# Sums of MLP weight blocks: VectorE's adds replaced by accumulating DMAs on GpSimd's queue

## The chip, the cores and the metric

The program runs on one core of a Trainium2 chip. The time is the device time of one execution in microseconds (us); smaller is better. Each run of a kernel gives one such time, and one further execution is recorded by the hardware profiler.

## The reference

One layer of an encoder on a sequence of 1024 positions and 1024 channels, all in float32. The change touches only its second half, the output projection, the MLP and the last norm:

```
x = x + g1 * (merged @ w_out)
h2 = rmsnorm(x, norm2_g) * (1 + sc2) + sh2
f = square(relu(h2 @ w_ff1)) @ w_ff2        # 1024 -> 4096 -> 1024
x = x + g2 * f
out = rmsnorm(x, final_g)
```

## The kernel before

**Phases.** The first half of the program (up to about 930 us) makes `merged`. The second half, `phase2`, is nine stages of 1024x1024 matrix products: stage 0 is `merged @ w_out`; then come four pairs, an "nl" stage (one quarter of `w_ff1`, then relu and square; stages 1, 3, 5, 7) and a "lin" stage (one quarter of `w_ff2`; stages 2, 4, 6, 8).

**Seven products in place of eight.** In stages 1 to 8 both operands are cut in 2x2 quadrants, and a Strassen-like scheme makes the result from seven quadrant products. For it the weight quadrants 11, 12, 21 and 22 are combined to four sums (`WSUM`): S1 = 21 + 22, S2 = S1 + 11, S3 = 11 + 21, S4 = S2 + 12 (signs are already in the weights). Each sum is made in two halves h = 0 and 1, as tiles of 128x1024 float32 (512 KB). That makes 4 sums x 2 halves x 8 stages = 64 adds, made by `w2_add` on VectorE (L105). The tiles are eleven buffers named `wr`. When `plan` says that an input isn't needed any more, the sum is written over it (40 of the 64); otherwise it goes to a free buffer (24).

**Granules.** A product is worked in two halves, called granules J here (`self.gran[J]`): 24 matmuls of 128x512. Stage 1 is J = 16 to 29, stage 2 is J = 30 to 43, and so on by 14, stage 8 is J = 114 to 127. Each operand is split in a high and a low part, since a product is made of three matmuls (high x high, high x low, low x high): ScalarE copies the tile to `whi` or `xhi`, then VectorE subtracts to get `wlo` or `xlo` (`w2_split`, `x2_split`). Each of these four has four buffers, so granule J's split can start when granule J - 4 is done.

**Order.** Each engine runs its instructions in program order. The loop at L1727 writes, for each granule G: its matmuls; the loads of weights that become possible (SyncE's queue); `w2_add` for the next granules; the sums of x (`x2_add`); `w2_split(G + 3)`; x splits; and `x2_load(G + 3)`. The x operands of stage 1 are also written to DRAM scratch `hop` by DMAs from GpSimd's queue (L1539), and stages 3, 5 and 7 load them back from there, on the same queue (L1546), two DMAs a granule. The residual x is saved to `xsp` by that queue, too (L1597). GpSimd waits for a DMA's semaphores before it issues it, so a DMA that waits holds up those behind it.

In stage 1, `S4` is the operand of granules 20 and 21, `S2` of 22 and 23, `S3` of 24 and 25, `S1` of 26 and 27. In stage 2 `S3` is that of 32 and 33, `S2` of 34 and 35.

Of the kernel before, what the change touches and what calls it, by code (L numbers as in the profile page):

```python
# [10 lines left out]
ALU = mybir.AluOpType  # L11
# [33 lines left out]
class Program:  # L45
# [1401 lines left out]
    def w2_add(self, J):  # L1447


        s, pos, h = self.gran[J]  # L1450
        f = self.wform.get((s, h), {})
        for n, st in enumerate((self.wplan[s][pos] or ((),))[0]):
            if st[0] == "sum" and (J, n) not in self.wdone:
                _, name, a, b, at, freed = st
                if not {a, b, at or name} <= f.keys() or {at, freed} & {self.wplan[s][q][1] for q in range(pos)
                                                                     if (s, q, h) not in self.wsplit}:
                    return False
                self.wdone.add((J, n))
                dst = f[at or name]
                self.add(dst, f[a], f[b])  # L1460
                f[name] = dst
                if freed:
                    self.rawfree.append(f[freed])
        return True
# [83 lines left out]
    def phase2(self):  # L1548
# [42 lines left out]
        def take_out(i):  # L1591

            k, t = ((0, 0), (1, 0), (1, 1), (0, 1))[i]
            for m in range(4):
                upd(0, k, t, m, banks[i % 2][m])
                square(t, k, m)
            self.G.dma_start(out=xsp[k][t], in_=xg[k][t].rearrange("p c n -> p (c n)"))  # L1597
# [66 lines left out]
        def squares():  # L1664
            while late:
                a, sq = late.pop()
                self.add(a, a, sq)
# [43 lines left out]
        at = {}  # L1711
# [14 lines left out]
        n_g = len(self.gran)  # L1726
        for G in range(-4, n_g - 2):  # L1727
            if G >= 0:
                s, pos, h = self.gran[G]
                if s == 0:  # L1730
                    if G and G % 4 == 0:
                        take_out(G // 4 - 1)
                    bank, begins, ends, skip = banks[G // 4 % 2], G % 4 == 0, G % 4 == 3, False
                else:
                    n, (kind, order) = 7 * (s - 1) + pos, self.STAGES[s]
                    if h == 0:
                        take(n - 1) if n else take_out(3)
                    i, bank = order[pos], banks[n % 2]
                    skip = pos > 1 and order[pos - 2] == self.GOES_ON[kind].get(i)
                    begins, ends = h == 0 and not skip, h == 1  # L1740
                (whi, wlo), (xhi, xlo) = self.wops[G % 4], self.xop[G % 4]
                for p in range(2):
                    if p:
                        for f in at.get((G, "mid"), ()):
                            f()
                    for m in range(4):
                        o = slice(p * 512 + m * 128, p * 512 + (m + 1) * 128)
                        for c, (w, x) in enumerate(((whi, xhi), (whi, xlo), (wlo, xhi))):
                            self.mm(bank[m], w[:, o], x[:, p, :], start=begins and p == c == 0,
                                    stop=ends and p == 1 and c == 2, skip=skip)  # L1750
                for f in at.get((G, "end"), ()):
                    f()
            squares()
            self.w2_loads(G + 8)
            for J in range(max(G + 1, 0), min(G + 5, n_g)):
                self.w2_add(J)
            for J in range(G + 1, min(G + 5, n_g)):
                if J >= 0 and self.x2_own(J) and not 20 <= J < 24 and self.x2_there(J) <= G:
                    self.x2_add(J)
            if G >= -3:  # L1760
                self.w2_split(G + 3)
            for J in range(G + 1, min(G + 4, n_g)):
                if J >= 0 and self.x2_own(J) and (not 20 <= J < 24 or G >= 19) and self.x2_there(J) <= G:
                    self.x2_split(J)
            if G >= -3:
                self.x2_load(G + 3)
            self.w2_loads(G + 8)
            if 8 <= G < 16 or G > 32 and self.STAGES[self.gran[G][0]][0] == "nl" and self.gran[G][1] > 1:
                for J in range(G + 5, min(G + 9, n_g)):
                    self.w2_add(J)  # L1770


        cuts = (slice(0, 256), slice(256, 512))
# [146 lines left out]
```

## Time and profile before

| | |
|---|---|
| median of 3 runs | 1677.84 us (1677.39 to 1680.4) |
| profiled execution, its own time | 1678.33 us |
| span of its trace | 1676.6 us |
| TensorE (PE) busy | 1635.8 us, 98% of the span |
| VectorE (DVE) busy | 1253.8 us, 75% |
| ScalarE (ACT) busy | 669.7 us, 40% |
| GpSimd (POOL) busy | 74.6 us, 4% |
| mean granted clock of TensorE | 0.993 of full speed |

The span is that of the trace; the execution's own time has 1.7 us around it. An engine that is busy 98% of the span bounds the kernel, and the rest of the span is read from the places where that engine waits. Times within the trace are counted from the span's start.

### The profile page before, as it was taken

The page shows a single profiled execution, that of the slowest core. Times are in us where ns is not written, and L with a number is a line of the kernel's source. Part 1 is how long each engine was busy: PE and PEld are TensorE (multiplying, and loading weights), DVE is VectorE, ACT ScalarE, POOL GpSimd, SP SyncE. Part 2 cuts the span into 40 slices and gives each one's busy share as a digit, 9 for nine tenths or more (in the row PEclk, how much of TensorE's full clock was granted, in tenths as well). Part 3 has the DMA queues.
Part 4 walks back from the last instruction along what each step waited for, and adds up shares of the span by engine and source line. Part 5 has one row for each costly group of instructions (what it writes and reads, how often), then busy time and mean ns, then how long its engine had stood idle before and what let it go on. Part 6 is the DMA issues. An engine that isn't in the chain of part 4 may idle for free.

```text
span 1676.6 us, 19562 instructions
## 1 busy us (share of the span) xinstructions
PE 1635.8 (98%) x7480; PEld 1350.6 (81%) x7480; DVE 1253.8 (75%) x1912; ACT 669.7 (40%) x876; POOL 74.6 (4%) x130
## 2 busy tenths in 40 slices
PE   6999999999999999999999999999999999999996
PEld 4888878888878888888888888777888888888885
DVE  8889787769877875455666649899559847974896
ACT  5433323554436537552221235643243334323443
POOL 0000000000000000000000001100110021012002
PEclk9999999999999999999999999999999999999998
DMA  8421435533545444054464624661571274157102
GB/s 318 170 88 63 132 107 149 181 136 110 167 145 195 156 170 151 26 188 141 186 240 174 255 97 188 238 233 44 212 274 39 91 252 175 51 171 261 58 1 101
DMA packets 84768, 257.05 MB, mean 153 GB/s; under 512 B 9921, under 2 KB 24385, under 8 KB 83650
## 3 DMA queue, kind: packets, MB, share of 16 engines
q1 hardware_dynamic: 62274, 175.05, 30.8%
q0 software_dynamic: 17792, 67.12, 10.8%
q10 hardware_dynamic: 4608, 13.63, 2.1%
q8 instruction: 59, 0.97, 0.2%
q14 instruction: 35, 0.29, 0.1%
HBM read 199.14 MB, written 54.53 MB: 151 GB/s over the span
## 4 chain that ended last, share of the span: by engine, by line
PE 81%; DVE 11%; issue 3%; ACT 2%; DMA 2%; SPq 1%; DVEq 0%; ACTq 0%
PE pm L91 58%; PE pb L91 22%; DVE xlo L105 2%; DVE wlo L105 2%; DVE xg L122 1%; DVE fr L105 1%; DVE wr L105 1%; DVE fr L122 1%; SPq L149 1%; DMA ada<-ada 1%; DVE s L126 1%; DMA u<-zs 1%; DVE ssacc L105 1%; PE pb L96 0%; DMA lx<-zr 0%
## 5 line engine op out<-in xcount | busy, mean ns | idle before, releaser
L91 PE MATMUL pm<-act,whi 128*128 128x512 f32 x2176 | 673.1, 392 | 2.4 <-ACT act L146 2.4
L91 PEld LDWEIGHTS pm<-act,whi 128*128 128x128 f32 x2176 | 406.1, 188 | 88.3 <-ACT act L146 3.6
L91 PE MATMUL pm<-act,wlo 128*128 128x512 f32 x1088 | 419.8, 389 | 0.0
L146 ACT ACTIVATE whi<-wr 128x1024 fp32r<-128x1024 f32 x124 | 131.0, 1057 | 298.1 <-PE pm L91 128.8
L91 PEld LDWEIGHTS pm<-act,wlo 128*128 128x128 f32 x1088 | 204.4, 188 | 43.0
L105 DVE TENSOR_TENSOR wlo<-wr,whi 128x1024 fp32r<-128x1024 f32 x124 | 151.3, 1221 | 114.1 <-ACT whi L146 114.1
L91 PE MATMUL pb<-xhi,whi 128*128 128x512 f32 (+1 forms) x512 | 200.6, 392 | 5.0 <-DVE fr L105 2.7
L91 PE MATMUL pm<-xlo,whi 128*128 128x512 f32 (+1 forms) x528 | 203.8, 386 | 1.5 <-DVE xlo L105 1.5
L91 PE MATMUL pm<-xhi,whi 128*128 128x512 f32 (+1 forms) x528 | 204.6, 387 | 0.0
L91 PE MATMUL pm<-xhi,wlo 128*128 128x512 f32 (+1 forms) x528 | 203.8, 386 | 0.0
L91 PE MATMUL pb<-xlo,whi 128*128 128x512 f32 (+1 forms) x512 | 199.5, 390 | 0.6 <-DVE xlo L105 0.6
L91 PE MATMUL pb<-xhi,wlo 128*128 128x512 f32 (+1 forms) x512 | 199.2, 389 | 0.0
L146 ACT ACTIVATE whi<-wraw 128x1024 fp32r<-128x1024 f32 x74 | 78.1, 1057 | 102.7 <-PE pm L91 85.6
L91 PEld LDWEIGHTS pb<-xhi,whi 128*128 128x128 f32 x512 | 97.5, 190 | 26.2 <-issue 3.8
L91 PEld LDWEIGHTS pm<-xlo,whi 128*128 128x128 f32 x528 | 99.2, 188 | 21.9 <-DVE xlo L105 1.9
L91 PEld LDWEIGHTS pm<-xhi,whi 128*128 128x128 f32 x528 | 99.2, 188 | 20.1 <-issue 0.2
L91 PEld LDWEIGHTS pm<-xhi,wlo 128*128 128x128 f32 x528 | 99.2, 188 | 20.1
L91 PEld LDWEIGHTS pb<-xlo,whi 128*128 128x128 f32 x512 | 97.5, 190 | 21.2 <-DVE xlo L105 1.0
L91 PEld LDWEIGHTS pb<-xhi,wlo 128*128 128x128 f32 x512 | 97.5, 190 | 19.7
L105 DVE TENSOR_TENSOR wlo<-wraw,whi 128x1024 fp32r<-128x1024 f32 x74 | 90.0, 1218 | 8.0 <-ACT whi L146 7.7
L105 DVE TENSOR_TENSOR wr<-wr,wr 128x1024 f32<-128x1024 f32 x64 | 77.5, 1219 | 0.6
L146 ACT ACTIVATE xhi<-fr 128x1024 fp32r<-128x1024 f32 x54 | 56.6, 1050 | 44.4 <-DVE fr L122 23.3
(265 smaller groups left out, 1908.2 us busy)
## 6 DMA issues: line engine op xcount, KB each, us to landing
wr<-w SPq DMA_DIRECT2D x76, 512.0 KB, 4.5
ada<-ada SPq DMA_DIRECT2D x48, 512.0 KB, 6.4
xhi<-hop POOLq DMA_DIRECT2D x42, 512.0 KB, 3.6
xlo<-hop POOLq DMA_DIRECT2D x42, 512.0 KB, 4.9
wraw<-wgate SPq DMA_DIRECT2D x32, 512.0 KB, 3.9
tg<-tg ACTq DMA_DIRECT2D x24, 512.0 KB, 2.9
tl<-tg SPq DMA_DIRECT2D x24, 512.0 KB, 5.6
wraw<-win SPq DMA_DIRECT2D x20, 512.0 KB, 3.6
```

The costliest lines, as they stand in the source:

```text
L91: self.P.matmul(out=out, lhsT=lhsT, rhs=rhs, start=start, stop=stop, skip_group_check=skip)
L105: self.V.tensor_tensor(out=out, in0=a, in1=b, op=op)
L122: self.V.scalar_tensor_tensor(out=out, in0=a, scalar=s, in1=b, op0=op0, op1=op1, **kw)
L126: self.V.tensor_tensor_scan(out=out, data0=a, data1=b, initial=0.0, op0=ALU.mult, op1=ALU.add)
L146: self.A.activation(out=out, in_=a, func=f, **kw)
L149: (self.S if q == "S" else self.A).dma_start(out=out, in_=a)
```

## The change

`w2_add` issues DMAs from GpSimd's queue in place of VectorE's add. When the sum goes to a free buffer, a plain DMA copies the first input there, and a second DMA adds the other input to it (`accum_op`). When it is written over an input, one accumulating DMA does it. So 64 adds become 64 accumulating DMAs and 24 copies. The loop also offers sums up to eight granules ahead always, in place of four ahead and eight in some granules only.

```diff
@@ w2_add
                 dst = f[at or name]
-                self.add(dst, f[a], f[b])
+                if at is None:
+                    self.G.dma_start(out=dst, in_=f[a])
+                self.G.dma_start(out=dst, in_=f[a if at == b else b], accum_op=ALU.add)
                 f[name] = dst
@@ the loop over granules
             self.w2_loads(G + 8)
-            for J in range(max(G + 1, 0), min(G + 5, n_g)):
+            for J in range(max(G + 1, 0), min(G + 9, n_g)):
                 self.w2_add(J)
...
             self.w2_loads(G + 8)
-            if 8 <= G < 16 or G > 32 and self.STAGES[self.gran[G][0]][0] == "nl" and self.gran[G][1] > 1:
-                for J in range(G + 5, min(G + 9, n_g)):
-                    self.w2_add(J)
```

GpSimd's queue where stage 0 ends and stage 1 begins, before: the third and fourth save of x (`xsp`), and the stores of the x operands of granules 16 to 19.

```order
L1597 DMA xsp_7359<-xg_7320 128x2048
L1539 DMA hop_7328<-xhi_7004 128x1024
L1539 DMA hop_7329<-xlo_7005 128x1024
L1539 DMA hop_7330<-xhi_7006 128x1024
L1539 DMA hop_7331<-xlo_7007 128x1024
L1539 DMA hop_7332<-xhi_7008 128x1024
L1539 DMA hop_7333<-xlo_7009 128x1024
L1597 DMA xsp_7357<-xg_7318 128x2048
L1539 DMA hop_7334<-xhi_7010 128x1024
L1539 DMA hop_7335<-xlo_7011 128x1024
```

The same place with the change, first piece, with the semaphores that a DMA waits for (`DMASW` is a DMA of this queue, `DMAHW` one of SyncE's). The rows at L1461 are copies, those at L1462 accumulate: S1 of half 0 in `wr_3`, S2 of half 0 in `wr_4`, S1 of half 1 in `wr_7`.

```order
L1599 DMA xsp_7359<-xg_7320 128x2048 [waits DMASW2_49,DVE_49]
L1461 DMA wr_3_7309<-wr_1_7307 128x1024 [waits DMAHW3_49,DMAHW4_49,DMAHW1_49,DMAHW5_49,DMAHW0_49,Activation_49]
L1462 DMA wr_3_7309<-wr_2_7308 128x1024 [waits DMAHW2_49,DMASW7_49]
L1461 DMA wr_4_7310<-wr_3_7309 128x1024 [waits DMASW0_49,Activation_49]
L1462 DMA wr_4_7310<-wr_8_7314 128x1024 [waits DMAHW5_49,DMASW1_49]
L1461 DMA wr_7_7313<-wr_5_7311 128x1024 [waits DMAHW3_49,DMAHW4_49,DMASW3_49,DVE_49]
L1462 DMA wr_7_7313<-wr_6_7312 128x1024 [waits DMAHW4_49,DMASW4_49,DMASW3_49]
L1541 DMA hop_7328<-xhi_7004 128x1024 [waits DMASW5_49,Activation_49]
```

Six DMAs now stand between the third save and the first `hop` store, and four of them wait for the one just ahead of them. After five more `hop` stores the second piece follows: the last save, S4 and S3 of half 0 (in `wr_7149` and `wr_8`), the stores of granule 19, and S2, S4 and S3 of half 1.

```order
L1599 DMA xsp_7357<-xg_7318 128x2048 [waits DVE_49]
L1462 DMA wr_7149<-wr_4_7310 128x1024 [waits DMAHW7_49,DMASW4_49]
L1462 DMA wr_8_7314<-wr_1_7307 128x1024 [waits DMASW5_49]
L1541 DMA hop_7334<-xhi_7010 128x1024 [waits DMASW6_49,Activation_49]
L1541 DMA hop_7335<-xlo_7011 128x1024 [waits DMASW7_49,DVE_49]
L1461 DMA wr_1_7307<-wr_7_7313 128x1024 [waits DMASW5_49,DMASW0_49]
L1462 DMA wr_1_7307<-wr_7148 128x1024 [waits DMAHW6_49,DMASW1_49,DMASW0_49]
L1462 DMA wr_0_7306<-wr_1_7307 128x1024 [waits DMAHW0_49,DMASW2_49,DMASW1_49]
L1462 DMA wr_7148<-wr_5_7311 128x1024 [waits DMASW3_49]
```

This queue uses eight semaphores in turn, so S4 of half 0 (first L1462 row) also waits for the DMA eight ahead of it, the accumulation of S1 of half 1. The copy for S2 of half 1 into `wr_1` waits until S3 of half 0 has read `wr_1`.

VectorE in stage 2, ahead of granules 33 and 34:

```order
 L122 SCALAR_TENSOR_TENSOR fr_7001<-fr_7001 128x512
-L105 TENSOR_TENSOR wr_0_7306<-wr_0_7306,wr_7148 128x1024
-L105 TENSOR_TENSOR wr_5_7311<-wr_0_7306,wr_5_7311 128x1024
 L105 TENSOR_TENSOR fr_6996<-fr_6996,fr_6998 128x1024
 L122 SCALAR_TENSOR_TENSOR fr_6998<-fr_6996,fr_7002 128x1024
 L105 TENSOR_TENSOR wlo_7238<-wr_8_7314,whi_7237 128x1024
 L105 TENSOR_TENSOR xlo_7007<-sp_7324,xhi_7006 128x1024
-L105 TENSOR_TENSOR wr_1_7307<-wr_1_7307,wr_3_7309 128x1024
-L105 TENSOR_TENSOR wr_7149<-wr_1_7307,wr_7149 128x1024
 L105 TENSOR_TENSOR fr_6997<-fr_6997,fr_6999 128x1024
```

S1 and S2 of both halves leave VectorE here, and nothing else moves on it; the adds for S3 stood a few rows ahead.

## Rows read from the trace of the kernel before

**Rows 1.** The page's first part: busy time and share of the span

```profile
PE 1635.8 (98%) x7480; PEld 1350.6 (81%) x7480; DVE 1253.8 (75%) x1912; ACT 669.7 (40%) x876; POOL 74.6 (4%) x130
```

**Rows 2.** TensorE's waits from 930 us on: total us, times, longest

```profile
PE pm L91 <- DVE xg L122: 4.4, 1, 4.4
PE pb L91 <- DVE fr L105: 2.7, 1, 2.7
PE pb L91 <- DVE xg L122: 2.3, 1, 2.3
...
PE pm L91 <- DVE xlo L105: 1.5, 1, 1.5
```

**Rows 3.** Stretches: length; PE, PEld, DVE, ACT, POOL busy (instructions); clock, DMA share, GB/s

```profile
1064.00:1080.00 16.00, 12.99 (x49) 10.28 (x50) 13.07 (x14) 13.56 (x20) 3.19 (x6) 0.89 0.47 168
...
1128.00:1150.00 22.00, 18.22 (x72) 14.26 (x71) 21.90 (x24) 9.09 (x9) 0.00 (x0) 0.92 0.16 48
1150.00:1600.00 450.00, 450.00 (x1987) 372.62 (x1986) 334.68 (x358) 159.43 (x182) 44.23 (x84) 1.00 0.43 150
```

**Rows 4.** VectorE's adds of weight blocks: in all, then from 1107 to 1137 us

```profile
L105 DVE TENSOR_TENSOR wr<-wr,wr 128x1024 f32<-128x1024 f32 x64 | 77.5, 1219 | 0.6
...
L105 DVE TENSOR_TENSOR wr<-wr,wr 128x1024 f32<-128x1024 f32 x6 | 7.3, 1220 | 0.1
```

**Rows 5.** TensorE in time: first matmuls of granules 33, 34, 35; one whole product

```profile
1128.86 0.39 PE L91 MATMUL pm<-xhi,whi 128*128 128x512 f32 x1
...
1138.54 0.47 PE L91 MATMUL pb<-xhi,whi 128*128 128x512 f32 x1 [2.30 <-DVE xg L122]
...
1145.70 0.39 PE L91 MATMUL pb<-xhi,whi 128*128 128x512 f32 x1
...
1151.31 10.88 PE pm L91 x48
```

**Rows 6.** VectorE in time, stage 2

```profile
1123.53 2.48 DVE L105 TENSOR_TENSOR wr<-wr,wr 128x1024 f32<-128x1024 f32 x2
...
1129.45 1.22 DVE L105 TENSOR_TENSOR xlo<-sp,xhi 128x1024 fp32r<-128x1024 f32 x1
...
1136.51 1.22 DVE L105 TENSOR_TENSOR xlo<-fr,xhi 128x1024 fp32r<-128x1024 f32 x1
```

**Rows 7.** GpSimd's queue in time: the third save of x

```profile
1015.48 0.53 POOL L1597 DMA_DIRECT2D xsp<-xg  x1 [27.69 <-DVE xg L122]
```

**Rows 8.** ScalarE in time: the high parts of granules 20 and 21

```profile
1039.77 1.05 ACT L146 ACTIVATE whi<-wr 128x1024 fp32r<-128x1024 f32 x1
...
1054.81 1.04 ACT L146 ACTIVATE whi<-wr 128x1024 fp32r<-128x1024 f32 x1
```

**Rows 9.** DMAs issued from 1012 to 1068 us: KB each, median us to landing

```profile
hop<-xhi POOLq DMA_DIRECT2D x7, 512.0 KB, 2.9
hop<-xlo POOLq DMA_DIRECT2D x7, 512.0 KB, 3.9
...
xsp<-xg POOLq DMA_DIRECT2D x2, 1024.0 KB, 4.1
```

**Rows 10.** The end: TensorE's transposes, VectorE's reduce, TensorE's long wait

```profile
1638.03 0.60 PE L96 MATMUL pb<-ident,nrm 128*128 128x128 f32 x4
...
1639.60 0.68 DVE L130 TENSOR_REDUCE ss<-pb 128x4 f32<-128x512 f32 x1
...
1647.21 2.08 PE L91 MATMUL pm<-nrm,ones 128*128 128x512 f32 x2 [4.41 <-DVE xg L122]
```

**Rows 11.** Around stage 5: a weight load, the first load of x; loads' median landing

```profile
1297.01 0.33 SPq L149 DMA_DIRECT2D wr<-w  x1
...
1331.12 0.53 POOL L1546 DMA_DIRECT2D xhi<-hop  x1 [80.55 <-PE pm L91]
...
wr<-w SPq DMA_DIRECT2D x76, 512.0 KB, 4.5
```

**Rows 12.** DMAs issued from 1090 to 1112 us: KB each, median us to landing

```profile
hop<-xlo POOLq DMA_DIRECT2D x3, 512.0 KB, 13.3
```

## The prediction

> **What bounds the kernel now.** I read the busy times first: TensorE works 98% of the span [rows 1], so a change on another engine can win only where TensorE waits. Its list of waits shows four that end with VectorE's work on x or the residual [rows 2]. The stretches place them: the first near 1064 us (2.7 us waited), two between 1128 and 1150 us (1.5 and 2.3), one at 1647 us (4.4). In the first two of these stretches the granted clock is below 1 as well (0.89 and 0.92): after a wait TensorE is slow for a while. From 1150 to 1600 us it is busy for all 450 us [rows 3]. So of 64 adds that take 77.5 us of VectorE [rows 4], the forty in stages 3 to 7 stand beside a TensorE that never waits, and taking them away is worth nothing there. Only the rest can count.
>
> **What is removed.** *Stage 2.* Between 1107 and 1137 us VectorE does six adds, 7.3 us [rows 4], and is busy 21.9 of the 22 us after 1128 [rows 3]: it is behind. TensorE begins granule 33 at 1128.86, then waits for its low part of x, which starts on VectorE at 1129.45, behind the two adds at 1123.53; granule 34 begins at 1138.54, after the low part of 1136.51 [rows 5, 6]. Granules 33 and 34 together take 1145.70 - 1128.86 = 16.84 us, and two granules at pace 10.88 [rows 5]: the wait and the slow clock behind it cost 5.96 us. Four adds stand ahead of the first late low part, 4 x 1.22 = 4.9 us, so it starts near 1124.6, ahead of 1128.86; all six stand ahead of the second, which starts near 1129.2, while granule 34 at pace begins at 1134.3. Both are then in time, by more than 3 us. I count the whole 5.96 us as won.
>
> *Stage 1.* The wait near 1064 us follows a chain on ScalarE and VectorE with no add in it; the three adds at its head give back about 0.9 us, if the sums come in time (below).
>
> *The end.* The transposes for the last norm are done at 1638.63, and VectorE's reduce begins only at 1639.60, since VectorE is late; the long wait that ends at 1647.21 lies behind it [rows 10]. Stage 8's S4 adds (2.4 us) stand ahead of the reduce. It can't start before the transposes: I count 0.9 us.
>
> **What is added.** 88 DMAs of 512 KB on GpSimd's queue. No row shows an accumulating DMA, nor one from SBUF to SBUF. Let c be the time of a copy from issue to landing, a that of an accumulation. For c the near rows are this queue's 512 KB stores in the stretch in question, 2.9 and 3.9 us [rows 9]; I take 3.7, as more traffic is added there. For a: not below the 2.9 of a plain store; 1 MB on the same queue takes 4.1 [rows 9], and an accumulation reads twice what it writes; the upper end is twice the slower store, 7.8. I take 5.0, nearest the 1 MB row, with 0.9 for the company.
>
> A page of the Trainium skill has a price for a: "Collectives: The Full Stack", in its part on why ReduceScatter is half of AllGather, says that the add in a DMA engine costs no time of its own, only a second source read on the same ring. An estimate by that page is a near 4.2 us, and the sum below would then show no loss at all in stage 1.
>
> The sums are needed late everywhere but in stage 1. There they form one chain in the queue (the second and third order pieces). It starts when the third save of x is issued, 1015.48 + 0.53 = 1016.0 [rows 7]:
> - copy and add for S1 of half 0, then copy and add for S2: the last add is issued at 1016.0 + 2c + a;
> - half a microsecond later the copy for S1 of half 1, then its add, which lands at 1016.5 + 3c + 2a;
> - S4 of half 0 waits for that add's semaphore (same one of eight), and S3 of half 0 is issued 0.5 us behind it: it lands at 1017.0 + 3c + 3a. The `hop` stores and the save that stand between take 7 x 0.53 us and pass in the time of that add;
> - S2 of half 1: its copy needs the buffer that S3 has read (+c), its add (+a), then S4 of half 1 (+a).
>
> S4 of half 1 lands at 1017.0 + 4c + 5a = 1017.0 + 14.8 + 25.0 = 1056.8. Granule 21's high part is made from it on ScalarE, in program order, at 1054.81 before [rows 8]. So it is 2.0 us late. Queued behind it on ScalarE and VectorE are the normed x, the sums of x and the split for granule 22, the chain at whose end TensorE already waits near 1064 us: the 2.0 us pass to it whole, and the 0.9 us of stage 1 are not won. (S4 of half 0 lands at 1016.5 + 3c + 3a = 1042.6, 2.8 us after 1039.77 [rows 8]; ScalarE waits for TensorE and VectorE shortly after that, which takes up nearly all of it.)
>
> Stage 2 has room: copies and adds for S3 begin near 1083 us, and the high part of granule 32 is made at 1111. In stages 3, 5 and 7 the x loads stand in the queue behind sums. Ahead of stage 5 the weight load issued at 1297.01 lands about 4.5 us later [rows 11], 1301.5; then three adds and three copies follow each other, 1301.5 + 3c + 3a = 1327.6, and the first x load was issued at 1331.12 [rows 11]. It is needed three granules (16.3 us) later. So there is no wait up to a = 9. The extra reach of the loop, up to eight granules ahead, only lets the queue begin early; it is priced in these times. GpSimd's own issue time (0.53 us each) lies on an engine that is 4% busy [rows 1].
>
> **The sum.** -5.96 (stage 2) - 0.9 (end) + 2.0 (stage 1) = -4.9 us on the profiled execution's own 1678.33, 1673.4. That execution stands 0.5 above the median of the runs, so **1673 us** is my forecast for the median.
>
> **The rivals.**
> 1. *The accumulation is slow and stage 1 pays for it.* The chain holds five of them, so each microsecond on a costs 5 us once it is late. Stage 1's loss is 4c + 5a - 37.8; with c = 3.7 it equals the 6.9 us won elsewhere at a = 6.0, and from a = 6.7 on the kernel is slower than can be mistaken. At a = 7.0 the loss is 12.0, the sum +5.1: 1683 us. At the upper end, 7.8, it is 16.0, the sum +9.1: 1687. For it: nothing shows that the adder keeps pace with a plain packet. Against it: in that stretch 1 MB lands in 4.1 us.
> 2. *A tie.* a between 5.3 and 6.7: stage 2's gain is paid back in stage 1 within 3.4 us. Time: 1678 us.
> 3. *Traffic eats stage 2's gain.* From 1090 to 1112 us `hop` stores take 13.3 us to land, where they took 3.9 before [rows 9, 12]: the residual and the weights are loaded then. Sums that queue there land late, and the x splits of granules 32 and 33 wait for the delayed stores; if that holds ScalarE 5 us, stage 2 stays as it is: +2.0 - 0.9, 1679 us. The page "DMA: Bandwidth & Descriptors" of the Trainium skill says, in its section on issuing engines, that DMAs of all engines run on the same 16 DMA engines and interleave; by that rule moving work to another queue buys no bandwidth, and rows 9 and 12 agree. Against it: the high parts have some 10 us until TensorE needs them.
> 4. *The fast end.* a = c = 2.9: S4 lands at 1043.1, stage 1 loses nothing and wins 0.9: -7.8, 1670 us.
> 5. *The adds leave VectorE, but stage 2 isn't freed*, since another wait ends there at the same time: with stage 1 in time, -1.8: 1676 us.
>
> **How the numbers follow.** The runs lie within about 0.2% of each other, 3.4 us; less can't be told from no change. My chances: forecast and rival 4 together 0.45 (0.33 and 0.12); rival 1 0.29; rivals 2, 3 and 5 together 0.26 (0.15, 0.07, 0.04), of which 0.02 may end slower. So faster 0.45, same 0.24, slower 0.31. The range goes from the fast end less 1 us, 1669, to rival 1's upper end, 1688, which leaves out the cases of a over 8 us. The forecast's own range is 1670 to 1674.5.
>
> **What would show it.** Right: the adds are gone from VectorE; granules 33 and 34 together take about 10.9 us at full clock; the wait near 1064 us is some 2 us longer, and ended by a DMA through ScalarE; accumulations land in about 5 us; 1150 to 1600 us stays without a wait. Wrong would be: accumulations over 6 us, a wait of TensorE at granule 21 or 22 that is 5 us or more longer, a first wait in stages 3, 5 or 7 ended by an x load, or granules 33 and 34 still waiting on VectorE.

## The result, and the profile after

| | before | after |
|---|---|---|
| median of 4 runs each | 1678.54 us (1677.39 to 1680.4) | 1723.68 us (1719.23 to 1725.1) |
| profiled execution, its own time | 1678.33 us | 1719.23 us |
| span of its trace | 1676.6 us | 1717.4 us |

The ratio is 1.0266, interval 1.0253 to 1.0278: the change made the kernel slower by 2.7%. I had forecast 1673, with a range that ended at 1688. The trace of the kernel after is that of the fastest of its four runs, so the spans differ by 40.9 us and the medians by 45.1.

The page's first part of the kernel after, which answers to [rows 1]:

```profile
PE 1645.0 (96%) x7480; PEld 1352.6 (79%) x7480; DVE 1185.0 (69%) x1848; ACT 669.5 (39%) x876; POOL 144.3 (8%) x218
```

VectorE did lose its 64 adds [rows 4]: its busy time fell from 1253.8 to 1185.0 us. GpSimd is still idle 92% of the time. TensorE's share fell all the same. Its waits from 930 us on, after (engine, line, what ended the wait: us in all, times, longest; [rows 2] before):

```profile
PE pm L91 <- ACT u L146: 12.0, 1, 12.0
PE pm L91 <- DMA xhi<-hop: 11.6, 3, 5.2
PE pb L91 <- DVE fr L105: 3.8, 1, 3.8
PE pm L91 <- DVE xg L122: 3.5, 1, 3.5
...
PE pm L91 <- DMA xlo<-hop: 2.3, 3, 1.0
```

The reader is to see two lines that were not in [rows 2]: one wait of 12.0 us that ends with ScalarE's `u`, and waits for loads of x from `hop`. Of the lines of [rows 2], that of `pb` with `xg` (2.3) is gone, but four new waits for `fr` in stage 2 (2.7 us in all) have come. That of `pm` with `xg` is 3.5 in place of 4.4: the 0.9 us of the end.

The DMA view after: GpSimd's queue, and the sums beside the loads of weights and x (KB each, median us to landing):

```profile
q0 software_dynamic: 30464, 113.26, 22.9%
...
wr<-wr POOLq DMA_DIRECT2D x88, 512.0 KB, 6.0
wr<-w SPq DMA_DIRECT2D x76, 512.0 KB, 6.7
...
xhi<-hop POOLq DMA_DIRECT2D x42, 512.0 KB, 8.3
```

The weight loads took 4.5 before [rows 11], the loads of x (`xhi<-hop`) 3.6. The loads of x are issued in stages 3, 5 and 7 and stand in the same queue as the sums.

**Where the time went.** The start of each granule's first matmul is in both traces; the difference of the two starts grows wherever the kernel after loses. In the granules that have no column in this table the difference does not change by 0.1 us. The rows below the first are the experiments of the next section, counted in the same way against the same trace of before; a minus is time won.

| us lost | ahead of stage 0 | stage 1, gr. 16 to 23 | stage 1 to 2, gr. 24 to 35 | stage 3, start (gr. 36 to 49) | stage 3, end | stage 5 | stage 7 | end | span |
|---|---|---|---|---|---|---|---|---|---|
| after | 1.5 | 17.3 | -0.2 | 4.0 | 8.7 | 8.3 | 2.4 | -1.0 | +40.9 |
| e1_hop_on_sync | -0.2 | 20.1 | 2.8 | 1.0 | 0.0 | 0.0 | 0.0 | -0.8 | +22.9 |
| e2_copy_for_add | 3.1 | 8.6 | -6.0 | 0.0 | 5.0 | 6.7 | 0.0 | -1.0 | +16.4 |
| e3_stage1_vector | 2.7 | 1.3 | -3.1 | 2.7 | 9.1 | 8.4 | 2.8 | -1.1 | +22.9 |
| e4_vector_reach | 3.1 | -0.3 | 7.3 | 0.0 | 0.0 | 0.0 | 0.0 | -0.1 | +10.0 |
| e5_first_part | 1.0 | 15.8 | 5.1 | 29.9 | 7.4 | 33.4 | 44.9 | -1.0 | +136.5 |
| e6_stages_2_and_8 | -0.7 | 1.6 | 2.7 | 0.0 | 0.0 | 0.0 | 6.6 | -1.3 | +8.9 |
| e7_s3_on_vector | 1.9 | 19.0 | -6.0 | 7.9 | 0.0 | 0.0 | 0.0 | -1.1 | +21.7 |
| e9_early_chain | 2.0 | 3.0 | -3.6 | 6.6 | 9.7 | 8.7 | 8.4 | -0.2 | +34.6 |
| e10_s124_of_2_and_8 | -0.9 | 1.6 | -6.0 | 0.0 | 0.0 | 0.0 | 0.0 | -1.1 | -6.4 |
| e11_same_earlier | -0.4 | 0.0 | 0.6 | 0.0 | 0.0 | 0.0 | 0.0 | -1.1 | -0.9 |
| e12_early_and_sync | 0.5 | 1.4 | 3.1 | 3.5 | 0.0 | 0.0 | 0.0 | -0.8 | +7.7 |

The first column differs by 4 us between traces in which nothing is changed there, so it is no effect; a stage's column holds nothing of it. Stage 1's column is 1.6, 1.6 and 0.0 in e6, e10 and e11, which change nothing in that stage, so a value under 2 us there is no effect either.

**Stage 1.** GpSimd's queue in time, after (start, time on GpSimd, what is issued, the idle time before it and what ended it; L1461 copies, L1462 accumulates, as in the order pieces):

```profile
1017.65 0.54 POOL L1461 DMA_DIRECT2D wr<-wr  x1 [0.16 <-issue]
1022.66 0.88 POOL L1462 DMA_DIRECT2D wr<-wr  x1 [4.47 <-DMA wr<-wr]
1027.98 0.55 POOL L1461 DMA_DIRECT2D wr<-wr  x1 [4.43 <-ACT xhi L146]
...
1037.33 0.85 POOL L1462 DMA_DIRECT2D wr<-wr  x1 [4.74 <-DMA wr<-wr]
1037.89 0.84 POOL L1541 DMA_DIRECT2D hop<-xhi  x1
...
1041.06 0.80 POOL L1599 DMA_DIRECT2D xsp<-xg  x1
1042.37 0.87 POOL L1462 DMA_DIRECT2D wr<-wr  x1 [0.51 <-DMA wr<-wr]
1043.90 0.87 POOL L1462 DMA_DIRECT2D wr<-wr  x1 [0.66 <-DMA hop<-xhi]
...
1058.73 0.54 POOL L1461 DMA_DIRECT2D wr<-wr  x1 [11.30 <-DMA wr<-wr]
```

The queue stands still until each input has landed. So six `hop` stores and the last save of x, which were issued from 1019.05 to 1035.04 before, are let go all at once from 1037.89 to 1041.06, 4 MB in all, and S4 and S3 of half 0 (1042.37 and 1043.90) are issued right behind them. Landing times from three narrow windows of the DMA view: first the third row above (a copy with nothing beside it) and the second (an accumulation alone), then S4 at 1042.37:

```profile
wr<-wr POOLq DMA_DIRECT2D x1, 512.0 KB, 2.9
...
wr<-wr POOLq DMA_DIRECT2D x1, 512.0 KB, 4.8
...
wr<-wr POOLq DMA_DIRECT2D x1, 512.0 KB, 13.2
```

The same accumulation takes 4.8 us alone and 13.2 behind the stores. ScalarE and then TensorE wait for it:

```profile
1055.69 1.06 ACT L146 ACTIVATE whi<-wr 128x1024 fp32r<-128x1024 f32 x1 [14.64 <-DMA wr<-wr]
1056.66 2.04 ACT L146 ACTIVATE u<-pm 128x512 f32<-128x512 f32 x4
...
1057.29 2.08 PE L91 MATMUL pm<-nrm,ones 128*128 128x512 f32 x2 [11.98 <-ACT u L146]
```

This is granule 20's high part (1039.77 before, [rows 8]). Four evictions of `u` stand behind it in ScalarE's program, and TensorE's matmul for the norm's sums needs these. That the wait is booked on `u` hides its cause; the idle time of the row before shows it.

**Stage 2.** The stores wait behind S3's copies, and the x splits wait for the stores (their buffers):

```profile
1111.89 0.81 POOL L1461 DMA_DIRECT2D wr<-wr  x1
1131.36 0.87 POOL L1462 DMA_DIRECT2D wr<-wr  x1 [18.66 <-DMA wr<-wr]
1131.92 0.85 POOL L1541 DMA_DIRECT2D hop<-xhi  x1
1132.46 0.85 POOL L1541 DMA_DIRECT2D hop<-xlo  x1
...
1142.01 1.23 DVE L105 TENSOR_TENSOR xlo<-sp,xhi 128x1024 fp32r<-128x1024 f32 x1 [8.35 <-DMA hop<-xlo]
```

S3 of half 1 is copied at 1111.89, while the residual's 4 MB and weights are loaded; the copy takes 19.2 us, the queue stands still for 18.66, two stores that were ready go out at 1131.92, and VectorE, free of its adds, idles 8.35 us for them.

**The ends of stages 3, 5 and 7.** The same queue, where the last x operands of stage 3 are loaded:

```profile
1256.77 0.53 POOL L1461 DMA_DIRECT2D wr<-wr  x1
1266.47 0.88 POOL L1462 DMA_DIRECT2D wr<-wr  x1 [9.17 <-DMA wr<-wr]
1267.03 0.86 POOL L1548 DMA_DIRECT2D xhi<-hop  x1
...
1268.08 0.87 POOL L1461 DMA_DIRECT2D wr<-wr  x1
1278.87 0.88 POOL L1462 DMA_DIRECT2D wr<-wr  x1 [9.92 <-DMA wr<-wr]
1279.43 0.87 POOL L1548 DMA_DIRECT2D xhi<-hop  x1
...
1287.93 0.76 PE L91 MATMUL pm<-xhi,whi 128*128 128x512 f32 x1 [5.20 <-DMA xhi<-hop]
```

The copies are S3 of stage 4, which is needed soon; each accumulation waits for its copy, and the x load of granule 56 is issued at 1279.43, 8.5 us ahead of the matmul that ends up waiting for it. At the start of stage 3 it is the same with the sums that stand there: nine of their DMAs are issued from 1171.51 on, five of which wait until another one of them has landed, and the first x load behind them is issued at 1207.85, where it was 1178.80 before.

### The profile page after: what moved, and what is told of

Same layout as the page of the kernel before. It is cut to its first block, busy times and chain, and to the rows that moved or that the text cites. A ratio compares the mean times of both kernels' runs of the same rounds, so it can differ in the third digit from the quotient of the medians.

```text
span 1717.4 us, 19727 instructions
## 1 busy us (share of the span) xinstructions
PE 1645.0 (96%) x7480; PEld 1352.6 (79%) x7480; DVE 1185.0 (69%) x1848; ACT 669.5 (39%) x876; POOL 144.3 (8%) x218
## 3 DMA queue, kind: packets, MB, share of 16 engines
q0 software_dynamic: 30464, 113.26, 22.9%
## 4 chain that ended last, share of the span: by engine, by line
PE 70%; issue 11%; DMA 8%; DVE 7%; POOL 2%; ACT 1%; SPq 0%; POOLq 0%; DVEq 0%; ACTq 0%
PE pm L91 52%; PE pb L91 18%; DMA xlo<-hop 2%; DMA wr<-wr 2%; DVE t L105 1%; DVE s L126 1%; DMA ada<-ada 1%; DMA xg<-xT 1%; DVE wlo L105 1%; DMA hop<-xlo 1%; PE pb L96 1%; DVE xg L122 0%; DVE v L105 0%; DMA lx<-zr 0%; DVE w L105 0%
## 5 line engine op out<-in xcount | busy, mean ns | idle before, releaser
L1462 POOL DMA_DIRECT2D wr<-wr x64 | 57.8, 927 | 271.5 <-DMA wr<-wr 155.9
```

The costliest lines, as they stand in the source:

```text
L1462: self.G.dma_start(out=dst, in_=f[a if at == b else b], accum_op=ALU.add)
```

## The experiments

Three theories stood against each other. The first, the theory of the order (Q): a sum waits in GpSimd's queue for its inputs, and what stands behind it is late. The rivals: the sums' bytes fill the 16 DMA engines, whatever the order (T); an accumulation is slow in itself (A). Where a kernel was run once, that one time is given; where it was run several times, the median with the ratio's interval. The median of the kernel before, measured beside them, was 1678.6 to 1678.8 in all of them.

**e1_hop_on_sync.** The other DMAs of GpSimd's queue go to SyncE's; the sums stay.

```diff
-                self.G.dma_start(out=self.hop[self.STAGES[s][1][pos], h, p], in_=flat(t).bitcast(F32))
+                self.S.dma_start(out=self.hop[self.STAGES[s][1][pos], h, p], in_=flat(t).bitcast(F32))
...
-            self.G.dma_start(out=xsp[k][t], in_=xg[k][t].rearrange("p c n -> p (c n)"))
+            self.S.dma_start(out=xsp[k][t], in_=xg[k][t].rearrange("p c n -> p (c n)"))
```

The loads from `hop` are changed in the same way.

> The sums stay accumulating DMAs on GpSimd's queue; the stores and loads of hop and the saves of x are issued from SyncE's queue. Theory Q (the loss comes from GpSimd's program order: a sum that waits holds up the x loads and stores behind it, which then pile up ahead of the next sum): the 4.0, 8.7, 8.3 and 2.4 us lost at granules 44 to 47, 56 and 57, 84 and 85, 110 and 111 vanish, and with c = 3.0 and a = 4.7 S4 of half 1 in stage 1 lands near 1053 us, so that most of the 17 us of stage 1 vanish too: 1680 us, give or take 5. Rival T (the 16 DMA engines are short of time for the added traffic, whichever queue issues it): 1712 to 1724 us. Rival A (the accumulation itself is slow): stage 1's loss stays, the x loads' waits stay in part: 1705 to 1720 us.

Measured: 1704.7 us, ratio 1.0174 (1.0149 to 1.0199), 20 us above the upper end that theory Q gave. The losses at the ends of stages 3, 5 and 7 are gone, with all 88 DMAs still there: for these the order is shown and the mere traffic ruled out. Stage 1 is as bad as before, which the order alone does not explain. GpSimd's rows there:

```profile
1022.09 0.55 POOL L1461 DMA_DIRECT2D wr<-wr  x1 [78.81 <-DMA wr<-w]
1031.57 0.90 POOL L1462 DMA_DIRECT2D wr<-wr  x1 [8.93 <-DMA wr<-wr]
```

The chain now begins 4.4 us later, since its weight loads now stand behind the third save of x in SyncE's queue and are issued only at 1015.45, and its first copy takes 9.2 us beside stores and loads in place of 4.7. Another queue brought no room there. The Trainium skill has a rule for this in "DMA: Bandwidth & Descriptors", section "Issuing engines are not separate DMA queues": DMAs of all issuing engines run on the same 16 DMA engines. This trace agrees, with the 9.2 us.

**e2_copy_for_add.** Every accumulation is a plain copy with the same waits; the addition is left out.

```diff
-                self.G.dma_start(out=dst, in_=f[a if at == b else b], accum_op=ALU.add)
+                self.G.dma_start(out=dst, in_=f[a if at == b else b])
```

> Each accumulating DMA is a plain DMA copy of the same input to the same place with the same waits, so the addition is left out. Rival A (the accumulation is slow): nearly all of the loss goes, under 1690 us. Theory Q: the waits and the order stay, each link of the chain is 1.6 us shorter (2.9 against 4.5 us alone) and a queued one 1.2 us: stage 1's loss falls by some 10 us, the loss at the x loads by a few: 1700 to 1710 us. Rival T (traffic): 64 x 512 KB less to read, a sixth of the queue's load: 1705 to 1715 us.

Measured: 1694.68 us (one run), less than theory Q and rival T gave and more than rival A did. Of the 40.9 us of the changed kernel 24.5 are gone: in this order of the queue the cost of accumulating makes up the larger part of the loss. It is not all of it. Of 17.3 us in stage 1 half stays, and stages 3 and 5 keep 5.0 and 6.7: a DMA as fast as a copy would still lose 8.6 - 6.0 + 5.0 + 6.7 - 1.0 = 13 us there.

**e3_stage1_vector.** Stage 1's sums back on VectorE.

```diff
+                if s == 1:
+                    self.add(dst, f[a], f[b])
+                else:
...
```

The two DMAs stand below the `else`, unchanged.

> The eight sums of stage 1 are VectorE's adds again, those of stages 2 to 8 stay DMAs. Theory Q: the 17 us lost between granules 18 and 23 vanish, the four losses at x loads (23 us together) stay, and stage 2's 6 us can be won or not, depending on the sums that queue beside the loads of x: 1695 to 1703 us. Rivals T and A: the same for stage 1; by T also a part of the later losses, 1690 us.

Measured: 1701.24 us (one run). Stage 1's loss is gone, and the losses in stages 3, 5 and 7 stay within some 1.5 us of what they were: these losses are separate and add up. Stage 2 wins 3.1 in place of 0.2.

**e4_vector_reach.** The change's second part alone: VectorE's adds, offered eight granules ahead always.

```diff
-                if at is None:
-                    self.G.dma_start(out=dst, in_=f[a])
-                self.G.dma_start(out=dst, in_=f[a if at == b else b], accum_op=ALU.add)
+                self.add(dst, f[a], f[b])
```

> All sums are VectorE's adds as before, offered up to eight granules ahead always: the second part of the change alone. All theories: the same adds at the same cost on VectorE, some of them earlier, in places ahead of work that TensorE waits for: 1675 to 1684 us. Above 1690 the change of the order alone would explain a good part of the loss.

Measured: 1688.4 us (one run), above what all theories gave; 3.1 us of it stand ahead of stage 0, and 7 us are lost in granules 30 to 35 alone. The reason is again a wait in program order: at 1114.54 VectorE starts an add of weight blocks after standing still for 9.08 us, until a load of weights has landed, and the work for granules 30 and 31 stands behind that add. So on VectorE the reach does harm in stage 2; for the DMAs it is the other way:

**e5_first_part.** The first part alone: DMAs, offered where the kernel before offered its adds.

```diff
-            for J in range(max(G + 1, 0), min(G + 9, n_g)):
+            for J in range(max(G + 1, 0), min(G + 5, n_g)):
...
+            if 8 <= G < 16 or G > 32 and self.STAGES[self.gran[G][0]][0] == "nl" and self.gran[G][1] > 1:
+                for J in range(G + 5, min(G + 9, n_g)):
+                    self.w2_add(J)
```

> The change's first part alone: accumulating DMAs, offered at the places of the kernel before (four granules ahead, eight where it was eight). The theory (place in GpSimd's queue): in stage 1 the order of the queue stays nearly the same, since there the kernel before also offers eight ahead, so granules 19 to 22 still lose 14 to 18 us; the ends of stages 3, 5 and 7 also offer eight ahead, so S3's copy and accumulation still stand ahead of x loads and granules 56 and 84 still lose 7 to 9 us each; stage 2's sums stand behind the hop stores, and granules 33 and 34 win 3 to 6 us. 1714 to 1724 us. The rival (the longer reach does the harm, as it did for VectorE's adds): most of the loss is gone, under 1700 us.

Measured: 1814.87 us (one run), 90 us over the higher of the two forecasts. Both theories had taken the reach for a matter of earlier or later. Where stage 3 begins, DMAs of sums now stand between the x loads:

```profile
1223.08 0.88 POOL L1548 DMA_DIRECT2D xhi<-hop  x1
...
1224.16 0.88 POOL L1461 DMA_DIRECT2D wr<-wr  x1
1233.86 0.88 POOL L1462 DMA_DIRECT2D wr<-wr  x1 [8.82 <-DMA wr<-wr]
1238.69 0.54 POOL L1461 DMA_DIRECT2D wr<-wr  x1 [3.95 <-DMA wr<-wr]
1241.82 0.85 POOL L1462 DMA_DIRECT2D wr<-wr  x1 [2.59 <-DMA wr<-wr]
1246.86 0.87 POOL L1462 DMA_DIRECT2D wr<-wr  x1 [4.18 <-DMA wr<-wr]
1247.40 0.88 POOL L1548 DMA_DIRECT2D xhi<-hop  x1
...
1254.01 0.76 PE L91 MATMUL pb<-xhi,whi 128*128 128x512 f32 x1 [14.65 <-DMA xhi<-hop]
```

Between two x loads the queue serves five DMAs of sums one after the other, 23 us, since each of the last four waits until the one ahead has landed. Such a place costs 28 to 32 us at the start of each of the three stages. The longer reach is what keeps the change from most of this.

**e6_stages_2_and_8.** The kernel before, with the sums of stages 2 and 8 by DMA (`if s in (2, 8):`), where I took it that no x load shares the queue.

> The kernel before with its reach, and only the sums of stages 2 and 8 made by DMAs (there no load of x stands in GpSimd's queue). The theory: nothing is lost in stages 1 and 3 to 7, granules 33 and 34 win 3 to 6 us and the end 1 to 2: 1671 to 1675 us. The rival (traffic of the sums slows the hop stores and weight loads of stage 2): no gain, 1678 to 1682 us.

Measured: 1687.24 us, ratio 1.006 (1.0046 to 1.0074): above both forecasts. ScalarE, high parts of granules 32 and 33:

```profile
1120.03 1.06 ACT L146 ACTIVATE whi<-wr 128x1024 fp32r<-128x1024 f32 x1 [9.57 <-DMA wr<-wr]
...
1128.68 1.07 ACT L146 ACTIVATE whi<-wr 128x1024 fp32r<-128x1024 f32 x1 [6.64 <-DMA wr<-wr]
```

S3 is the first sum that stage 2 needs, and its copy stands behind the last `hop` stores, among the reload of the residual. I had also overlooked that stage 8's S3 is offered while stage 7's last x loads are in the queue (6.6 us).

**e7_s3_on_vector.** The changed kernel, S3 alone back on VectorE (`if name != "S3":` around the DMAs).

> The changed kernel with S3 alone back on VectorE. The theory: S3 of the next stage is what stands ahead of x loads at the ends of stages 3, 5 and 7; without it the x loads of granules 55, 56, 83 and 84 are issued as soon as TensorE has left their buffers, and granules 56 and 84 lose under 2 us in place of 8.7 and 8.3; stage 1 keeps most of its 17 us, less some 3 since S3 of half 0 leaves the chain. 1700 to 1708 us. The rival (the 16 DMA engines are full there, whatever stands in the queue): granules 56 and 84 still lose 5 us or more each, 1712 us or more.

Measured: 1700.05 us (one run). Ends of stages 3, 5 and 7: nothing lost; the x load of granule 56 is issued as TensorE leaves its buffer again:

```profile
1266.90 0.53 POOL L1551 DMA_DIRECT2D xhi<-hop  x1 [4.39 <-PE pm L91]
```

It was issued at 1279.43 in the changed kernel, at nearly the same loss up to there (22.8 and 22.6 us). Stage 2 wins 6.0. Two things I had not expected: stage 1 did not get better (19.0), and the start of stage 3 got worse (7.9 in place of 4.0), where the first x load still stands behind S1 and S2, issued at 1207.16.

**e9_early_chain.** The changed kernel with weights and sums offered earlier in stage 0.

```diff
-            self.w2_loads(G + 8)
-            for J in range(max(G + 1, 0), min(G + 9, n_g)):
+            self.w2_loads(G + (12 if 4 <= G < 16 else 8))
+            for J in range(max(G + 1, 0), min(G + (13 if 4 <= G < 16 else 9), n_g)):
```

> The changed kernel, with weights and sums offered twelve granules ahead in granules 4 to 15 in place of eight: S1 and S2 of half 0 stand ahead of the third save of x, four DMAs of the chain are then done before it. The theory (stage 1 loses by a chain of DMAs that begins too late): the chain ends some 12 to 18 us earlier, and granules 19 to 22 lose 0 to 5 us in place of 17; the rest stays: 1704 to 1714 us. The rival (stage 1 loses since the sums share the DMA engines with the hop stores and the save): the loss stays above 10 us, 1717 us or more.

Measured: 1712.94 us (one run). Stage 1 loses 3.0 in place of 17.3: S1 and S2 of half 0 are made from 990 us on, the first six `hop` stores go out from 1024.14 to 1029.88, and granule 20's high part starts at 1042.60:

```profile
1042.60 1.06 ACT L146 ACTIVATE whi<-wr 128x1024 fp32r<-128x1024 f32 x1 [1.06 <-DMA wr<-wr]
```

The sums still share the engines with stores and save, so sharing alone does not make the loss: what stage 1 lost came of a chain that began too late, and of the stores that its waits held back.

**e10_s124_of_2_and_8.** The kernel before, and by DMA only S1, S2 and S4 of stages 2 and 8: 12 accumulations, no copies.

```diff
-                self.add(dst, f[a], f[b])
+                if s in (2, 8) and name != "S3":
+                    if at is None:
+                        self.G.dma_start(out=dst, in_=f[a])
+                    self.G.dma_start(out=dst, in_=f[a if at == b else b], accum_op=ALU.add)
+                else:
+                    self.add(dst, f[a], f[b])
```

> The kernel before with its reach; in stages 2 and 8 alone S1, S2 and S4 by DMAs, all S3 and the other stages on VectorE. The theory: what spoiled stage 2 when S3 went there by DMA too was that S3, operand of granules 32 and 33, stood in GpSimd's queue behind hop stores and landed at 1119.95 and 1128.60; S1 and S2 are operands of granules from 34 on and have some 10 us more. So no load of x waits in stage 7, granules 33 to 35 win 2 to 6 us and the end 2 to 3: 1670 to 1675 us. The rival (the residual's reload and the weight loads set stage 2, so that S2 is late there as well): granule 34 or 35 waits through ScalarE for a DMA, 1678 us or more.

Measured: **1671.95 us**, ratio 0.9963 (0.9949 to 0.9976): 0.4% faster than the kernel before, which is little, but the interval excludes 1. TensorE's first matmuls of granules 33, 34 and 35, which answer to [rows 5], and VectorE's low part of x for granule 33, which started at 1129.45 in [rows 6]:

```profile
1129.54 0.39 PE L91 MATMUL pm<-xhi,whi 128*128 128x512 f32 x1
...
1134.98 0.39 PE L91 MATMUL pb<-xhi,whi 128*128 128x512 f32 x1
...
1140.42 0.39 PE L91 MATMUL pb<-xhi,whi 128*128 128x512 f32 x1
...
1126.11 1.22 DVE L105 TENSOR_TENSOR xlo<-sp,xhi 128x1024 fp32r<-128x1024 f32 x1
```

Two granules take 10.88 us, the pace of [rows 5]; 5.96 were forecast as won and 6.0 are.

**e11_same_earlier.** As e10, and these sums also offered up to eight granules ahead. In this order S1 of stage 2 overwrites an input of S3 before S3 is made, so S3 is added up from that sum in place of the weight block; the operations and their sizes are the same.

> As the run with S1, S2 and S4 of stages 2 and 8 by DMAs, but these sums are also offered up to eight granules ahead. The theory: S1 of both halves then stands between the hop stores, some 5 to 10 us earlier, and granule 34's sum is in time in any case: 1669 to 1674 us, the same as that run or up to 2 us faster. The rival (whatever is put between the hop stores delays x splits that wait for these stores): granules 31 to 33 lose 2 us or more, 1676 us or more.

Measured: 1677.86 us, ratio 0.9996 (0.9988 to 1.0005). TensorE loses 4.6 at granules 32 and 33 and wins 4.0 behind them. That is the rival's number by another way: VectorE's adds for S3 wait for the DMA of S1 that now stands ahead of them:

```profile
1111.61 1.22 DVE L105 TENSOR_TENSOR wr<-wr,wr 128x1024 f32<-128x1024 f32 x1 [2.83 <-DMA wr<-wr]
...
1120.23 1.23 DVE L105 TENSOR_TENSOR wr<-wr,wr 128x1024 f32<-128x1024 f32 x1 [3.99 <-DMA wr<-wr]
```

So it says nothing on earlier sums as such; a version with the right order was not tried.

**e12_early_and_sync.** The changed kernel with e1's and e9's edits together.

> The changed kernel, all 88 DMAs kept, with both remedies: weights and sums twelve granules ahead in granules 4 to 15, and the hop stores, hop loads and saves of x on SyncE's queue. The theory (the loss is a late chain in stage 1 and x loads that stand behind sums): of the 1704.7 us with the second remedy alone some 14 to 18 go away, 1686 to 1692 us. The rival (the sums' traffic itself costs the rest): 1697 us or more.

Measured: 1686.69 us, ratio 1.0047 (1.0034 to 1.0061), as the theory said. With all 88 DMAs and their additions kept, two changes of order take away 33 of the 41 us, so the traffic and the cost of accumulating by themselves make up at most the other 8. At the start of stage 3, 3.5 us remain, where TensorE still waits for loads of x. What remains in stage 2 is S3 again, as in e6: ScalarE's high part of its second half starts at 1138.90 and has waited 18.03 us for the sum.

## Why the prediction was wrong

**What held.** The adds left VectorE. The end won its 0.9. Stage 2's gain of 5.96 was right in place and size as soon as nothing late stood in its way (e2, e7, e10: 6.0). The prices were near for a DMA with nothing beside it: c = 3.7 against 2.9, a = 5.0 against 4.5 to 4.8. The estimate of 4.2 for a by the Trainium skill, page "Collectives: The Full Stack", part on why ReduceScatter is half of AllGather, was near as well: the measured accumulation takes 1.6 to 1.9 us more than the copy of the same size.

**What did not, in sum.** Stage 1 lost 17.3 us where 2.0 was forecast, stages 3, 5 and 7 together 23.4 where nothing was, and stage 2 won 0.2 where 5.96 was.

**The step that failed: stage 1's chain, and in it the price of an accumulation behind the stores.** S4 of half 0 was to land at 1042.6, and its lateness was to vanish in ScalarE's own waits. It was issued at 1042.37 and landed at 1042.37 + 13.2 = 1055.6. Granule 20's high part waited for it, and behind that stood the four evictions of `u`, which the prediction did not have: 14.3 of the 17.3 us are lost there, ahead of granule 19. I wrote that the stores and the save that stand between "take 7 x 0.53 us and pass in the time of that add". They were issued in that time, but their 4 MB were still on the way when S4 and S3 of half 0 were issued, which then took 13.2 and 14.3 us where I had a = 5.0. I had priced each DMA of the chain with company of 0.9 us, and had not asked where the stores go that its waits hold back: into the chain's own way. The rest follows: S3 of half 0 was to land at 1043.1 and landed at 1043.90 + 14.3 = 1058.2; S2 of half 1, which waits for it, was issued at 1058.73, and S4 of half 1 at 1067.87, where I had 1017.0 + 4c + 4a = 1051.8.

**The second: stages 3, 5 and 7 at nothing.** "There is no wait up to a = 9" came from one place, the sums ahead of stage 5's first x load, and there it held. The sums at the start of stage 3 cost 4.0 us, and I did not walk through the rest of the queue, where S3 of the next stage stands ahead of the last x loads. "GpSimd's own issue time lies on an engine that is 4% busy" was the wrong quantity: a GpSimd that waits for a landing blocks what stands behind, however little it is busy. The Trainium skill says where such a wait sits in "DMA: Bandwidth & Descriptors", section "Anatomy of one DMA": a semaphore wait happens on the issuing sequencer before dispatch. The trace agrees, with 18.66 us of standing still in one row.

**The third: stage 2.** "Stage 2 has room" took S3 to be made from 1083 us on. S3 of half 1 was copied at 1111.89 and its accumulation issued at 1131.36, and the `hop` stores behind it kept VectorE waiting.

**The fourth: the reach.** "Only lets the queue begin early" hid two effects, both large: 7 us lost with VectorE's adds (e4), and some 96 us saved for the DMAs (span of e5 less that of after).

**The rivals.** Rival 3, which I gave 0.07, named what stage 2 did: x splits that wait for delayed stores, no gain there. Rival 1 had the sign, and my sign for it, accumulations over 6 us, came: over the whole kernel the 64 accumulations took 4.5 to 14.3 us to land, with a median of 6.6. But it put one slow a on all five links of stage 1's chain. In that stage six of the eight took 4.6 to 7.7 and the two behind the stores 13.2 and 14.3, and 23.4 us are lost in stages where it had nothing. In e12 the accumulations are no faster (their median is 7.5), and the kernel loses 7.7: what a slow landing costs goes by what waits for it.

**Still open.** How stage 1's loss divides between the late start, the cost of accumulating and the 4 MB of stores: e2 halves it, e9 takes nearly all of it away, and the shares overlap. Why stage 7 lost 2.4 in the changed kernel and 8.4 in e9.

## What to carry to other kernels

A DMA that waits for its input on an in-order queue holds up everything behind it, however idle the engine, as an add that waits does on VectorE (e4); so list what stands behind each such DMA to the end of the program, not only at the place with the longest chain. Dependent DMAs take a landing each (here 2.9 and 4.5 us at the least), and what they held back comes out in one burst ahead of the next link. Move work off a busy engine only in the stage where that engine ends the waits: here twelve of the 64 sums gave the whole gain (e10).

## What the runs showed of the hardware

- An accumulating DMA of 512 KB within SBUF landed in 4.5 to 4.8 us with nothing or little beside it, a copy in 2.9 (both in stage 1's chain). Its issue takes GpSimd 0.87 us in place of 0.54; in e2 the copies at the same places take 0.54.
- Behind 4 MB of stores on the same queue the same accumulation took 13.2 us; in a stretch in which 4 MB of the residual and weights are loaded on another queue, a copy took 19.2.
- The time that the packets of GpSimd's queue took of the 16 DMA engines, before and in e2, where all 88 DMAs of the sums are copies (after is shown above):

```profile
q0 software_dynamic: 17792, 67.12, 10.8%
...
q0 software_dynamic: 30464, 113.26, 18.2%
```

That is 181 us of a span of 1676.6 before, 308 us of 1692.9 in e2, and 393 us of 1717.4 after, for the same bytes as in e2. As an estimate from these, a copy took 127 / 88 = 1.4 us of all 16 engines and the addition another 85 / 64 = 1.3, so an accumulation about twice as much as a copy. Whatever the queue's other DMAs were slowed by the sums is counted in.
